# The first layer's input projection as float32 products of unsplit weights and streams

## The chip, the core and the metric

The kernel runs on one core of one Trainium2 chip. The metric is the device time of one execution in microseconds, the median of several runs. The core's engines have queues of their own: PE (TensorE, matmuls; PEld is its weight load), DVE (VectorE), ACT (ScalarE), POOL (GpSimd) and SP (SyncE, which here only issues DMAs). Each engine takes its instructions in the order in which the program holds them, and waits for the data of the one at its head.

## The reference

Two streams, the latent one (512 tokens) and the context (256 tokens), of 1024 channels pass two layers. Of a layer only this matters here:

```python
ul = split_cols(modulate(rms_norm(h_l, norm1_g[i]), m_l[0], m_l[1]) @ w_in[i])
uc = split_cols(modulate(rms_norm(h_c, norm1_g[i]), m_c[0], m_c[1]) @ w_in[i])
# four mixers on slices of the 2696 columns: SSD, Hyena, retention, S5
y_l = jnp.concatenate([ssd_l, hy_l, ret_l, s5l], axis=-1) @ w_out[i]
h_l = h_l + m_l[2] * y_l
h_l = h_l + m_l[5] * swiglu(modulate(rms_norm(h_l, norm2_g[i]), m_l[3], m_l[4]), ffn_w_up[i], ffn_w_down[i])
```

The m are the modulation, six vectors of 1024 channels that a product of a condition with `mod_w` gives. All is float32. The context takes the same path in the first layer; in the second it only feeds the mixers.

## The kernel before

The streams lie with channels on partitions, eight tiles of 128 channels by 512 or 256 tokens. Large products are made as three float32r matmuls: operand and weight are each split into a high part, which float32r carries, and a low part, the rest (`split`: the high part is a copy on ACT, line 155, the low part a subtraction on DVE, line 134, or on POOL for some), and `mm3` multiplies high by high, high by low and low by high, summed in one bank of PSUM. All matmuls go through `mm`, line 126, so rows are told apart by their tiles. `ahl`, `alol` are the normed latent stream, `ahc`, `aloc` the context, `whi`, `wlo` the weights; `wd` is the small weight of the eight dt columns, high and low side by side.

A weight comes in pieces of 128 columns: `piece` loads 512 KB by SP (line 207) into a staging tile `wst` of 4 KB a partition, and `weights` splits two pieces into a pair of tiles, tags "wh" and "wl" of the pool `whl`, two places of 8 KB a partition for each tag. The staging ring "st" has three places. The modulation of the first layer (`mod`) loads its own weights (`wm`, two pieces for each 256 columns) through the same ring and multiplies straight from it; its sums need the PSUM ring "md", which has one bank and is also used by the S5 blocks.

The input projection goes by 11 blocks of columns, in the first layer in the order s5, hz, sb, sx, sz, h0, h1, rk, rv, rq, rg: ten of 256 columns and sb, with 128 and dt. `start` norms the inputs by pairs of channel tiles as their modulation arrives, loads the first two blocks' weights (through a staging ring of its own, "stw") and begins their products; `in_proj` does the others for both streams, and from the sixth block on places two or four tiles of columns of the modulation beside each block. `in_s`, `in_h` and `in_r` take the sums out of PSUM and send them to DRAM, from where the mixers read them. s5 is multiplied in halves of 256 tokens, rv with the stream as the stationary operand and 256 columns of weights as the moving one.

The order of the instructions is made by a planner that runs before the kernel does: each has a priority, and the planner places an instruction on its engine when its own model of the chip has it ready. Products of the projections have a priority 300000 later (`bulk`), so that the mixers' matmuls go first. Filters of Hyena, S5, SSD, Hyena, and retention of the context run beside the projection; the output projection begins after them with weights `wo` and tiles `yhl`, `yhc`.

Of the kernel before, what the change touches and what calls it, by code (L numbers as in the profile page):

```python
# [33 lines left out]
def halves(a):  # L34
    """A table as two float32 parts that float32r carries exactly."""
    def keep12(x):
        u = np.ascontiguousarray(x, np.float32).view(np.uint32).astype(np.uint64)
        return ((u + 2047 + ((u >> 12) & 1)) >> 12 << 12).astype(np.uint32).view(np.float32)
    hi = keep12(a)
    return np.ascontiguousarray(np.stack([hi, keep12(a - hi)], 1))  # L40
# [66 lines left out]
class Kern:  # L107
# [7 lines left out]
    def at(self, p):  # L115
        """Instructions in this block get priorities from p on."""
# [44 lines left out]
    def pst(self):  # L161
        """A PSUM bank from the ring of the current flow of work."""
# [5 lines left out]
    def pst2(self, fl="mm+xb"):  # L168
        """As pst, from two rings in turn where no mixer runs."""
        with self.flow(fl):  # L170
            return self.pst()
# [4 lines left out]
    def flow(self, fl, p=None):  # L176
        """Work that takes its banks and small tiles from rings of its own; p: its priority."""
# [10 lines left out]
    def rsq(self, v, n):  # L188
        """v: (128, n) tile, replaced by 1/sqrt(v)."""
# [13 lines left out]
    def piece(self, src, nk, ncol):  # L203
        """src: (128, nk * ncol) of a weight laid out by pieces."""
        pool, tag = self.stage
        st = pool.tile([128, 1024], F32, tag=tag, name="wst", bufs=2 if tag == "stw" else 3)[:, :nk * ncol]
        self.nc.sync.dma_start(st, src)
        return st.rearrange("p (k n) -> p k n", k=nk)

    def weights(self, srcs, nk=8):  # L210
        """Pieces of 128 columns as high and low parts."""
# [7 lines left out]
    def held(self, src):  # L219
        """Four tiles of rows of a weight with all its columns, src: (8, 128, 512)."""  # L220
# [12 lines left out]
    def proj(self, ps, W, c0, m, a, nk=8, order=None):  # L233
        hi, lo = W
# [6 lines left out]
    def bulk(self):  # L241
        """Products that fill the tensor engine come after the mixers' own."""
# [10 lines left out]
    def run(self):  # L253
        nc, tc, A = self.nc, self.tc, self.A
        es = ExitStack()
        with es:
# [7 lines left out]
            self.stage = self.wst, "st"  # L264
            self.body()
# [11 lines left out]
    def put_y(self, s, k, t, c0=0):  # L277
        """Keep tile k of the mixers' output: as operands of the output projection where these have room already."""
# [12 lines left out]
    def ytiles(self, s, p):  # L291
        """Tiles that are not written in the order of their making: each has its own place."""
# [41 lines left out]
    def mod(self, i, c0, c1):  # L334
        """Columns 256*c0 .. 256*c1 of the modulation of layer i."""
# [15 lines left out]
    def mod_vec(self, i, cols, both, p):  # L351
        """As mod for tiles of columns, with a column of the weights a row: products and sums on VectorE.
        The context stream has the tiles in both only."""
# [16 lines left out]
    def gains(self, i, part, s, gat):  # L370
        """(1 + scale) * g for a stream; part is 1 or 4."""
# [4 lines left out]
    def sq_acc(self, s, x, acc, first):  # L376
        """acc += x*x"""
# [7 lines left out]
    def rinv_rows(self, s, accs, scale, c0=0, c1=None):  # L385
        """Per-token 1/sqrt(scale * sum over channels + eps), broadcast to all partitions in PSUM."""
# [14 lines left out]
    def segs(self, s):  # L401
        """Ranges of tokens that are normed one after the other, so that products of one hide the norm of the next."""
# [23 lines left out]
    def start(self):  # L426
        """Norm of the inputs and the first two blocks of columns of the first layer's input projection,
        by pairs of channel tiles as their modulation arrives."""
# [5 lines left out]
        for s in streams:  # L434
            s.a = self.atiles(s)
# [21 lines left out]
        for j in range(4):  # L457
# [5 lines left out]
            if j < 2:  # L463
                self.stage = self.xp, "stw"
                self.in_weights(0, j)
                self.stage = self.wst, "st"
# [3 lines left out]
            for s, jj in ([(sc, 0)] if j == 0 else [(sc, 1), (sl, 0), (sl, 1)] if j == 1 else [(sc, j), (sl, j)]):  # L470
# [4 lines left out]
                for k in range(2 * jj, 2 * jj + 2):  # L475
                    t = self.tile_t(s, "nt")
                    self.mul(t, self.x[s.name][k], pbs[s.name])
                    self.act(t, t, AF.Identity, bias=m[:, k, s.mi:s.mi + 1], scale=g[:, k:k + 1])
                    hi, lo = s.a[0][k], s.a[1][k]
                    self.act(hi, t)  # L480
                    self.sub(lo, t, hi, None if k % 2 else nc.gpsimd)
# [18 lines left out]
    def sirens(self, i, streams, p):  # L500
        """Hidden features of the filters of layer i at all lags: even lags on the first 64 partitions, odd on the rest."""
# [23 lines left out]
    def filters(self, i, s, p, hid):  # L525
        """Spectra of the two filters of layer i for sequence length s.L; kept in DRAM."""
# [7 lines left out]
        for o in range(2):  # L534
# [30 lines left out]
            # the spectra stay unnormalised; the bias is scaled to match  # L565
# [36 lines left out]
    def conv3(self, out, ps, i, wat, step, tl, bat, n):  # L602
        """out = w0 x[t-1] + w1 x[t] + w2 x[t+1] + b from a projection in PSUM."""
# [5 lines left out]
    def hyena(self, i, s, p, F):  # L609
# [14 lines left out]
        for o in range(2):  # L624
# [14 lines left out]
            for ft in range(nft):  # L639
# [3 lines left out]
                for par in range(2):  # L643
                    ps = self.pst()
                    for cs in range(2):
                        # par 0: Ec | Es ; par 1: Os | Oc
# [22 lines left out]
                # P+ = [Pc | Ps] in t1 ; P- = [Ps' | Pc'] in t3  # L669
# [16 lines left out]
            for c in range(2):  # L686
# [3 lines left out]
                for par in range(2):  # L690
                    # par 0: Q1 C + Q2 S ; par 1: Q3 S + Q4 C
# [21 lines left out]
    def early(self, p):  # L713
        """What the S5 matrices of the first layer are made of, later the tables of the retention."""
        return p.tile([128, 32 * self.S_END], F32, tag="early", name="early")

    def causal(self, t, r, nh, fill):
        """Keep i >= j (r = 0) or i <= j (r = 1) of (j, h, i)."""
# [28 lines left out]
    def ret(self, i, s, p):  # L747
# [13 lines left out]
        # states of the chunks  # L761
# [17 lines left out]
        # running states, kept block-diagonal over the two heads of a tile  # L779
# [72 lines left out]
    def ssd(self, i, s, p):  # L852
# [18 lines left out]
        # token-major  # L871
# [14 lines left out]
        # ln dt - acs of the column's token, per (dir, head)  # L886
# [7 lines left out]
        for c in range(nch):  # L894
# [27 lines left out]
            # within the chunk  # L922
# [36 lines left out]
        for c in range(nch):  # L959
            cs = slice(128 * c, 128 * c + 128)  # L960
            # from the states that enter, with the directions on the two halves
# [847 lines left out]
def layout(inputs):  # L1809
    """The inputs in the order in which the kernel reads them."""  # L1810
    g = {n: np.asarray(a) for n, a in inputs.items()}
    A = {}
# [90 lines left out]
```

## Time and profile before

| | |
|---|---|
| median of 3 runs | 1917.36 us (1913.35 to 1920.76) |
| the profiled execution: span | 1919.5 us |
| PE busy over the span | 1790.1 us, 93% |
| PE busy from 46 to 500 us | 396.8 of 454 us |
| DVE busy from 46 to 500 us | 338.1 us |

The profile is of one execution. Its times count from its first instruction, its span is the time between the first and the last, and it lies 2.1 us above the median of the runs. Busy time of PE is the union of its matmuls, whose ends are modelled and overlap. The granted clock is the share of the full clock that TensorE got, 1 at 2.4 GHz and 0.5 at 1.2 GHz.

### The profile page before, as it was taken

What the parts mean: (1) busy time and instruction counts of PE and PEld (TensorE: products, weight loads), DVE (VectorE), ACT (ScalarE), POOL (GpSimd) and SP (SyncE); (2) the same over time, 40 slices, a digit from 0 to 9 for tenths busy, and PEclk for the clock granted to TensorE, in tenths of its full rate; (3) what the DMA queues carried; (4) which work ended last, traced back from release to release, by engine and by line L of the source; (5) the groups of instructions that cost most, each with busy time, mean ns of one, the idle gap of its engine ahead of it and who ended that gap; (6) DMA issues with size and microseconds to landing.
All of it is one profiled execution on the core that took longest, in us unless ns stands there. A gap on an engine that the chain in (4) does not pass through costs nothing.

```text
span 1919.5 us, 28992 instructions
## 1 busy us (share of the span) xinstructions
PE 1790.1 (93%) x10792; PEld 1526.3 (80%) x10792; DVE 1257.5 (66%) x2941; ACT 713.5 (37%) x1390; POOL 207.3 (11%) x273
## 2 busy tenths in 40 slices
PE   3789878898999999999999999989999999999997
PEld 2678767686789888888888989878866888888886
DVE  8788764778858899777665427678576843233336
ACT  4354234555227223212132115514673542222222
POOL 0201121123002000011223000121110000000000
PEclk9899979998899999999999999999997999999998
DMA  6656588765612335656635513565563322222331
GB/s 231 178 138 186 149 180 229 243 192 160 203 56 89 121 123 164 219 190 230 210 113 131 155 44 123 158 207 159 153 201 96 126 73 94 89 96 88 97 101 56
DMA packets 193089, 280.87 MB, mean 146 GB/s; under 512 B 51745, under 2 KB 127837, under 8 KB 192436
## 3 DMA queue, kind: packets, MB, share of 16 engines
q1 hardware_dynamic: 107188, 166.20, 28.5%
q10 hardware_dynamic: 55920, 64.72, 10.9%
q0 software_dynamic: 29840, 48.09, 8.9%
q8 instruction: 85, 1.39, 0.3%
q14 instruction: 56, 0.46, 0.1%
HBM read 235.00 MB, written 43.96 MB: 145 GB/s over the span
## 4 chain that ended last, share of the span: by engine, by line
PE 58%; DVE 11%; issue 8%; DMA 8%; ACT 3%; POOL 1%; ACTq 0%; SPq 0%; DVEq 0%; POOLq 0%
PE ps_mm L126 31%; PE ps_xb L126 20%; PE ps_xa L126 4%; DMA mvw<-in_wmt_dram 4%; PE ps_md L126 2%; DMA wst<-in_wi_dram 1%; ACT L155 1%; DVE mvo L364 1%; DVE wlo L134 1%; DVE gt L134 1%; DVE t L134 1%; DVE g L1499 1%; DVE cst L134 1%; DVE s5tmp L134 1%; ACT whi L155 1%
## 5 line engine op out<-in xcount | busy, mean ns | idle before, releaser
L155 ACT ACTIVATE whi<-wst 128x1024 fp32r<-128x1024 f32 (+3 forms) x226 | 198.9, 917 | 361.5 <-PE ps_mm L126 169.4
L134 DVE TENSOR_TENSOR wlo<-wst,whi 128x1024 fp32r<-128x1024 f32 (+3 forms) x226 | 233.9, 1058 | 83.5 <-ACT whi L155 81.2
L126 PE MATMUL ps_mm<-alol,whi 128*128 128x512 f32 (+1 forms) x688 | 262.7, 383 | 0.4 <-POOL alol L134 0.4
L126 PE MATMUL ps_mm<-ahl,wlo 128*128 128x512 f32 (+1 forms) x688 | 262.3, 382 | 0.0
L126 PE MATMUL ps_mm<-ahl,whi 128*128 128x512 f32 (+1 forms) x688 | 260.9, 383 | 0.3 <-ACT ahl L155 0.2
L126 PE MATMUL ps_mm<-h,whi 128*128 128x512 f32 (+1 forms) x592 | 168.8, 365 | 0.9 <-DVE h L134 0.7
L126 PE MATMUL ps_xb<-ahl,whi 128*128 128x512 f32 (+1 forms) x416 | 154.2, 373 | 3.8 <-ACT ahl L155 3.8
L126 PE MATMUL ps_xb<-ahl,wlo 128*128 128x512 f32 (+1 forms) x416 | 153.8, 370 | 0.0
L126 PE MATMUL ps_xb<-alol,whi 128*128 128x512 f32 (+1 forms) x416 | 153.5, 371 | 0.1
L134 DVE TENSOR_TENSOR sg<-sg,ps_mm 128x512 f32<-128x512 f32 (+1 forms) x70 | 39.9, 570 | 172.9 <-PE ps_mm L126 172.7
L126 PEld LDWEIGHTS ps_mm<-alol,whi 128*128 128x128 f32 x688 | 130.7, 190 | 26.4 <-issue 2.7
L126 PEld LDWEIGHTS ps_mm<-ahl,wlo 128*128 128x128 f32 x688 | 130.7, 190 | 24.5 <-issue 1.1
L126 PEld LDWEIGHTS ps_mm<-ahl,whi 128*128 128x128 f32 x688 | 130.2, 191 | 25.0 <-issue 1.6
L126 PE MATMUL ps_xb<-h,whi 128*128 128x256 f32 (+1 forms) x592 | 129.2, 310 | 0.1
L364 DVE SCALAR_TENSOR_TENSOR mvo<-mvw,crow 128x1024 f32<-128x1024 f32 x80 | 97.8, 1222 | 39.6 <-DMA mvw<-in_wmt_dram 38.7
L126 PE MATMUL ps_mm<-ahc,whi 128*128 128x256 f32 x368 | 107.4, 296 | 13.0 <-ACT whi L155 8.6
L126 PEld LDWEIGHTS ps_mm<-h,whi 128*128 128x128 f32 x592 | 103.7, 188 | 17.5 <-DVE h L134 1.2
L126 PE MATMUL ps_mm<-aloc,whi 128*128 128x256 f32 x368 | 108.2, 295 | 1.0 <-DVE aloc L134 1.0
L126 PE MATMUL ps_mm<-ahc,wlo 128*128 128x256 f32 x368 | 107.1, 293 | 2.0 <-DVE wlo L134 2.0
L126 PEld LDWEIGHTS ps_xb<-h,whi 128*128 128x128 f32 x592 | 98.9, 188 | 11.6 <-issue 1.1
L126 PE MATMUL ps_mm<-h,wlo 128*128 128x512 f32 (+1 forms) x296 | 107.9, 365 | 0.0
L155 ACT ACTIVATE h<-sg 128x512 fp32r<-128x512 f32 (+1 forms) x70 | 37.4, 534 | 161.7 <-DVE sg L134 161.6
(576 smaller groups left out, 4137.3 us busy)
## 6 DMA issues: line engine op xcount, KB each, us to landing
wst<-in_wu_dram SPq DMA_DIRECT2D x88, 512.0 KB
mvw<-in_wmt_dram POOLq DMA_DIRECT2D x56, 512.0 KB, 3.7
wst<-in_wi_dram SPq DMA_DIRECT2D x42, 512.0 KB
wst<-in_wm_dram SPq DMA_DIRECT2D x40, 512.0 KB
wst<-in_wd_dram SPq DMA_DIRECT2D x24, 384.0 KB
ftab<-in_c_ftL_dram POOLq DMA_DIRECT2D x32, 256.0 KB, 5.0
wst<-in_wd_dram SPq DMA_DIRECT2D x32, 256.0 KB
s5rot<-s5r SPq DMA_DIRECT2D x32, 192.0 KB
```

Of the source, the lines that this page charges most:

```text
L126: return self.nc.tensor.matmul(out, lhsT, rhs, start=start, stop=stop)
L134: return (eng or self.nc.vector).tensor_tensor(out, a, b, op=op)
L155: return self.nc.scalar.activation(out, in_, func, bias=bias, scale=scale)
L364: self.nc.vector.scalar_tensor_tensor(o, st, 1.0, crow[:, q], op0=ALU.mult, op1=ALU.mult, accum_out=mv[:, c, q:q + 1])
L1499: nc.vector.tensor_tensor_scan(o, dcy, x, 0.0, ALU.mult, ALU.add)
```

## The change

In the first layer the normed streams are no longer split: the norm's activation writes eight float32 tiles for each stream (the pool `ap` has 8 tiles of each instead of 16). The weights of the input projection are not split either: `plain` loads each piece by SP straight into one of the four places of the tags "wh" and "wl", taken in turn, with no staging. `proj` then makes one float32 product for each tile of rows. The dt weights become one padded tile of 64 columns in a place of its own. The second layer is as before, and the ring "stw" is gone.

```diff
+    def plain(self, srcs):
+        self.nplain += 1
+        w = self.whl.tile([128, 8, 256], F32, tag=("wh", "wl")[self.nplain % 2], name="wpl")
+        for h, src in enumerate(srcs):
+            self.nc.sync.dma_start(w[:, :, 128 * h:128 * h + 128], src.rearrange("p (k n) -> p k n", k=8))
+        return w
...
     def proj(self, ps, W, c0, m, a, nk=8, order=None):
+        if len(a) == 1:
+            with self.bulk():
+                for k in range(nk):
+                    self.mm(ps, W[:, k, c0:c0 + m], a[0][k], k == 0, k == nk - 1)
+            return
...
-            s.a = self.atiles(s)
+            s.a = [[self.ap.tile([128, s.L], F32, tag="a" + s.name, name="af" + s.name) for _ in range(8)]]
...
-                self.stage = self.xp, "stw"
                 self.in_weights(0, j)
-                self.stage = self.wst, "st"
...
-                    self.act(t, t, AF.Identity, bias=m[:, k, s.mi:s.mi + 1], scale=g[:, k:k + 1])
-                    hi, lo = s.a[0][k], s.a[1][k]
-                    self.act(hi, t)
-                    self.sub(lo, t, hi, None if k % 2 else nc.gpsimd)
+                    self.act(s.a[0][k], t, AF.Identity, bias=m[:, k, s.mi:s.mi + 1], scale=g[:, k:k + 1])
...
-        self.Ws[q] = self.weights([wi[:, 8 * o:8 * o + 1024] for o in range(off, off + ncol - 127, 128)])
+        self.Ws[q] = (self.weights if i else self.plain)([wi[:, 8 * o:8 * o + 1024] for o in range(off, off + ncol - 127, 128)])
...
+                            o = ps[:, 256 * j:256 * j + 256]
+                            if i == 0:
+                                self.mm(o, s.a[0][k][:, cs], W[:, k, :], k == 0, k == 7)
+                                continue
...
+        if i == 0:
+            self.nplain += 1
+            wd = self.wd = self.whl.tile([128, 8, 256], F32, tag=("wh", "wl")[self.nplain % 2], name="wdp")[:, :, 0:64]
+            self.nc.gpsimd.memset(wd, 0.0)
+            for r in range(2):
+                self.act(wd[:, :, 32 * r:32 * r + 4], st[:, :, 4 * r:4 * r + 4])
+            return
...
+                if i == 0:
+                    self.mm(ps[0:64, :n], self.wd[:, k], s.a[0][k], k == 0, k == 7)
+                    continue
...
+        if i == 0:
+            self.ts(dt, ps[0:64, :n], self.dtb[i], op0=ALU.add)
+        else:
+            self.act(t1, ps[64:128, :n])
+            self.stt(dt, ps[0:64, :n], self.dtb[i], t1, ALU.add, ALU.add)
...
-            self.ap = aps.enter_context(tc.tile_pool(name="ap", bufs=16, reuse_waits="tile"))
+            self.ap = aps.enter_context(tc.tile_pool(name="ap", bufs=16 if i else 8, reuse_waits="tile"))
```

## Rows read from the trace of the kernel before

**Rows 1.** Busy time (share of the span) and instructions, the page.

```profile
...
PE 1790.1 (93%) x10792; PEld 1526.3 (80%) x10792; DVE 1257.5 (66%) x2941; ACT 713.5 (37%) x1390; POOL 207.3 (11%) x273
...
```

**Rows 2.** Busy by stretch: PE, PEld, DVE, ACT, POOL, clock, DMA share, GB/s.

```profile
...
100.00:225.00 125.00, 118.12 (x749) 98.95 (x748) 107.56 (x250) 61.14 (x122) 14.66 (x15) 0.99 0.60 161
225.00:300.00 75.00, 53.74 (x317) 43.70 (x319) 44.95 (x100) 22.36 (x46) 14.42 (x19) 0.77 0.82 189
300.00:350.00 50.00, 46.45 (x317) 37.48 (x309) 27.07 (x51) 28.14 (x49) 5.76 (x6) 1.00 0.81 225
350.00:375.00 25.00, 21.25 (x164) 17.79 (x166) 21.27 (x43) 15.26 (x42) 9.15 (x10) 0.86 0.64 208
...
46.00:500.00 454.00, 396.82 (x2641) 327.89 (x2634) 338.14 (x773) 204.12 (x427) 84.10 (x92) 0.91 0.66 183
...
457.00:498.00 41.00, 32.43 (x236) 25.46 (x234) 35.01 (x107) 15.06 (x34) 5.86 (x10) 0.74 0.49 153
...
```

**Rows 3.** Busy time in stretches, of instructions on whi alone.

```profile
...
249.00:278.60 29.60, 0.00 (x0) 0.00 (x0) 0.58 (x1) 1.06 (x1) 0.66 0.61 168
...
```

**Rows 4.** SP's issues in order; its waits (225 to 300): total, times, longest.

```profile
...
270.34 0.34 SPq L207 DMA_DIRECT2D wst<-in_wi_dram  x1
...
SPq L207 <- PE ps_md L126: 10.4, 2, 9.9
...
```

**Rows 5.** PE's waits from 30 to 480 us: total, times, longest.

```profile
...
PE ps_xa L126 <- DVE rv L152: 9.1, 1, 9.1
PE ps_mm L126 <- ACT whi L155: 8.6, 1, 8.6
PE ps_xb L126 <- ACT sE L155: 5.5, 1, 5.5
...
PE ps_mm L126 <- ACT ahc L155: 4.0, 2, 3.4
...
```

**Rows 6.** Matmuls by tiles, 46 to 458 us: busy, mean ns, idle before.

```profile
...
L126 PE MATMUL ps_mm<-ahl,whi 128*128 128x512 f32 x136 | 56.3, 414 | 0.1
...
L126 PE MATMUL ps_mm<-ahc,whi 128*128 128x256 f32 x136 | 41.1, 312 | 13.0 <-ACT whi L155 8.6 <-ACT ahc L155 4.0 <-DVE BC L152 0.5
...
L126 PE MATMUL ps_mm<-whi,ahl 128*128 128x256 f32 x32 | 9.4, 301 | 0.0
...
L126 PE MATMUL ps_mm<-ahl,wd 128*128 128x512 f32 x8 | 3.3, 415 | 0.0
...
```

**Rows 7.** PE in order of time (start us, us); the matmuls that read glw.

```profile
...
103.12 0.39 PE L126 MATMUL ps_mm<-alol,whi 128*128 128x512 f32 x1
...
105.87 0.39 PE L126 MATMUL ps_mm<-alol,whi 128*128 128x512 f32 x1
...
204.15 0.28 PE L126 MATMUL ps_mm<-aloc,whi 128*128 128x256 f32 x1
...
205.80 0.28 PE L126 MATMUL ps_mm<-ahc,whi 128*128 128x256 f32 x1
...
282.89 0.59 PE L126 MATMUL ps_xa<-s5fy,glw 128*128 128x256 f32 x2
...
283.44 0.28 PE L126 MATMUL ps_mm<-aloc,whi 128*128 128x256 f32 x1
...
L126 PE MATMUL ps_xa<-s5fy,glw x40: 377/379/795, 282.9 to 1382.2; 128*128 128x256 f32 x40
...
```

**Rows 8.** Splits of the weights to 432 us: duration min/median/max, first and last.

```profile
...
L155 ACT ACTIVATE whi<-wst x21: 1041/1057/1062, 22.3 to 404.8; 128x1024 fp32r<-128x1024 f32 x21
...
L134 DVE TENSOR_TENSOR wlo<-wst,whi x21: 1193/1224/2185, 24.4 to 405.9; 128x1024 fp32r<-128x1024 f32 x21
...
```

**Rows 9.** PE by time: first and last projection product, first output product.

```profile
...
46.61 0.80 PE L126 MATMUL ps_mm<-ahc,whi 128*128 128x256 f32 x2
...
456.89 0.28 PE L126 MATMUL ps_mm<-ahc,wlo 128*128 128x256 f32 x1
...
498.21 0.79 PE L126 MATMUL ps_mm<-yhl,whi 128*128 128x512 f32 x1
...
```

More of the change, by code (lines that the diff above doesn't have):

```diff
@@ L205, in piece @@
         pool, tag = self.stage
-        st = pool.tile([128, 1024], F32, tag=tag, name="wst", bufs=2 if tag == "stw" else 3)[:, :nk * ncol]
+        st = pool.tile([128, 1024], F32, tag=tag, name="wst", bufs=3)[:, :nk * ncol]
         self.nc.sync.dma_start(st, src)
         return st.rearrange("p (k n) -> p k n", k=nk)
+    def plain(self, srcs):
[4 more added lines that the diff above has]
+        return w
     def weights(self, srcs, nk=8):
@@ L264, in run @@
             self.stage = self.wst, "st"
+            self.nplain = 0
             self.body()
@@ L1015, in in_weights @@
         wi = self.A["wi"][i]
-        self.Ws[q] = self.weights([wi[:, 8 * o:8 * o + 1024] for o in range(off, off + ncol - 127, 128)])
+        self.Ws[q] = (self.weights if i else self.plain)([wi[:, 8 * o:8 * o + 1024] for o in range(off, off + ncol - 127, 128)])
         if nm == "sb":
-            self.dt_weights(wi[:, 8 * (off + 128):8 * (off + 136)])
+            self.dt_weights(i, wi[:, 8 * (off + 128):8 * (off + 136)])
     def in_part(self, i, q, s):
@@ L1089, in in_r @@
                         for k in range(8):
-                            self.mm3(ps[:, 256 * j:256 * j + 256], s.a[0][k][:, cs], s.a[1][k][:, cs],
+                            o = ps[:, 256 * j:256 * j + 256]
+                            if i == 0:
+                                self.mm(o, s.a[0][k][:, cs], W[:, k, :], k == 0, k == 7)
+                                continue
+                            self.mm3(o, s.a[0][k][:, cs], s.a[1][k][:, cs],
                                      W[0][:, k, :], W[1][:, k, :], k == 0, k == 7)
@@ L1118, in in_r, with dt_weights @@
             self.out_raw(s.drk[:, at + c], t)
-    def dt_weights(self, src):
+    def dt_weights(self, i, src):
         st = self.sm.tile([128, 8, 8], F32, tag="dtw", name="dtw", bufs=1)
         self.nc.sync.dma_start(st, src.rearrange("p (k n) -> p k n", k=8))
+        if i == 0:
[5 more added lines that the diff above has]
+            return
         wd = self.wd = self.whl.tile([128, 8, 256], F32R, tag="wh", name="wd")[:, :, 0:128]
@@ L1156, in ssd_in @@
         nc.sync.dma_start(scanm, A["c_scan"][:, :n])
-        self.act(t1, ps[64:128, :n])
-        self.stt(dt, ps[0:64, :n], self.dtb[i], t1, ALU.add, ALU.add)
+        if i == 0:
[3 more added lines that the diff above has]
+            self.stt(dt, ps[0:64, :n], self.dtb[i], t1, ALU.add, ALU.add)
         self.act(t1, dt, AF.Abs)
```

## The prediction

> **What bounds the kernel now.** I read the page first [rows 1]: over its 1919.5 us span PE is busy 93%. That share mixes two things, so the second view cuts the span into stretches [rows 2]. The change touches only the first layer's input projection, whose products lie on PE from 46.6 to 457 us [rows 9], so the stretch to look at is 46 to 500. There PE is busy 396.8 of 454 us: it idles 57.2 us and holds a granted clock of 0.91. The reader should see that the loss is uneven. From 225 to 300 PE is busy only 53.7 of 75 us at clock 0.77; at the two levels of 1.2 and 2.4 GHz a mean of 0.77 means 46% of that stretch, 34.5 us, at the lower one. DVE has 338 of 454 us, and in 300 to 350 only 27.1 of 50. So the stretch is mostly bound by PE, with a hole in the middle and a tail (457 to 498) in which DVE is busy 35.0 of 41 us.
>
> The hole is what matters. Between 249 and 278.6 us PE runs not one product that reads a weight tile whi [rows 3]. The code and the queue of SP say why. The staging ring "st" has three places, shared by the modulation weights (wm) and the projection weights (wi). wm loads take the places first; the modulation's products must wait for the one PSUM bank of ring "md", which the S5 blocks use too. Until then the ring is full of wm: SP stands 10.4 us waiting for PE's ps_md products, and the next wi load is issued at 270.3 [rows 4]. PE then waits 8.6 us for the split of that weight [rows 5].
>
> **Added: longer products.** The projection has 136 products of 512 columns, 168 + 64 of 256, and 8 + 8 for dt, each now issued as three float32r matmuls (dt: two). The lines view has 136 for ahl and 136 for ahc in ring mm, 32 for the S5 halves of the latent stream [rows 6]; the remaining 64 = 32 + 16 + 16 stand in like rows: 1136 matmuls in all. Start to start, a 512-column float32r matmul takes (105.87 - 103.12) / 12 = 0.229 us over a run of twelve, so 0.6875 a product; a 256-column one (205.80 - 204.15) / 14 = 0.118 over fourteen, 0.354 a product [rows 7]. The price of a float32 product is on the trace too: the GLU's weight glw and its stream are float32, and its 20 products (three ranges of tokens in the first layer, two in the second, by two tiles of columns and two of rows) show as 40 matmuls, two each. From the first of two at 282.89 to 283.44 there are those two and one float32r matmul: 0.55 - 0.118 = 0.432 us for one float32 product of 256 columns [rows 7]. No float32 product of 512 columns is in the trace. From above I bound it by twice that, 0.864, since nothing that is paid once a matmul can double; from below by the ratio that float32r shows between the two widths, 0.432 x 0.229 / 0.118 = 0.84. I take 0.864; the lower bound would make the sum 3 us smaller.
> - 136 x (0.864 - 0.6875) = 24.0 us
> - 232 x (0.432 - 0.3536) = 18.2 us
> - dt: 8 x (0.864 - 0.458) + 8 x (0.432 - 0.236) = 4.8 us
>
> Together +47 us of PE at full clock. The Trainium skill (FP8 and Floating Point Precision, TensorE Precision Notes) speaks against the change more strongly: true FP32 takes four passes through the array. By it every product would cost 4/3 of today's three; the trace has 0.432 against 0.354 at 256 columns, 1.22 times. By the page the 512-column products, which the trace doesn't show, would add another 136 x (0.917 - 0.864) = 7 us to the sum; it is a rival below.
>
> **Removed on DVE, ACT and POOL.** 21 splits of weight pieces: 1.06 us on ACT and 1.22 us on DVE each [rows 8], 22 and 26 us. The 16 casts of the normed streams on ACT and their 16 subtractions on DVE and POOL go as well. dt loses one ACT copy and two small subtractions, its DVE add stays. All of it lies beside PE work except at these places:
>
> Start. Four of the 21 DVE splits (4 x 1.22 = 4.9 us), those of the first two blocks, come from 24.4 us on [rows 8], ahead of the norm's rv, for which PE waits 9.1 us [rows 5]. They come off that chain. From there to 100 us PE waits 4.0 us for ahc [rows 5]; the norm's activation now writes the operand itself, so I take 3 back. **-8** (bounds -5 and -11).
>
> Hole. Weights go straight from DRAM to four places of 8 KB (tags wh and wl, two each), one place a column block, dt's padded columns taking one. The load of a block waits for the products of the block four tiles earlier, not for st. So the blocks after h0 no longer wait for the modulation. The 21.3 us of idle time in 225 to 300 contain the 8.6 for whi, which goes; the rest are waits of the S5 chain (KT through DRAM, gt), which stay where the program's order puts PE behind them. I take 14. With products to run PE would also keep its clock: the 34.5 us at the lower level, of which it is busy 53.7 / 75, some 24.7, lose half of that, 12.4; I take 10. **-24** (bounds -8.6, the one direct wait, and -34).
>
> Elsewhere from 100 to 457. PE waits 5.5 us for sE, an activation queued on ACT behind the split of a weight that had just landed [rows 5], and the stretch 350 to 375 has clock 0.86 [rows 2], 7 us at the lower level, worth 3. With 1.5 of the 6.9 us that PE idles in 100 to 225: **-10** (bounds 0 and -14).
>
> Tail. Today's last projection product starts at 456.9, the first of the output projection at 498.2 [rows 9]; between them PE runs what is left of Hyena, SSD and the context's retention at clock 0.74, behind DVE (35.0 of 41 us) [rows 2]. Hyena and SSD need blocks (h1 above all) that the hole holds back to 278 us and later. If they are there earlier, their DVE work moves into 300 to 350, where DVE has 23 us free. I take half of the tail's DVE work, 17.5, with its little idle time: **-18** (bounds 0 and -30). This is the least certain term.
>
> DMA. Bytes are the same, but a load now lands in eight runs of 512 B a partition instead of one of 4 KB. DMA's share is 0.66 in this stretch [rows 2]. Lower bound nothing, since a load has up to three blocks' time; upper, one more late load like the 8.6 us one. I take 0. SP issues the same 21 loads, with no staging wait, but a load whose place is still read stands at the head of SP with the S5 loads (KT, s5U) behind it: a rival. The smaller pool of streams (8 tiles instead of 16) can only take waits away from the retention's pools laid over it: 0.
>
> **Sum.** 47 - 8 - 24 - 10 - 18 = -13 us. The profiled execution spans 1919.5 us, 2.1 above the median of 1917.4 and inside the three runs (1913.4 to 1920.8), so I take the difference to the median: **1904 us**. What runs after 500 us is not touched.
>
> **Rivals.**
> - The tail does not move (its chains are latencies, or they wait for rq and rg, which still come last): 47 - 8 - 24 - 10 = +5, 1922 us, within 0.5%. For it: retention of the context starts only when the last product has freed the streams. Against: DVE, not latency, fills the tail. Chance 0.25.
> - Slower: PE's instruction order is fixed beforehand, and the longer products do not land in the hole but ahead of mixers' matmuls that are ready. Then only the direct wait of 8.6 comes back there and the tail stays: 47 - 8 - 8.6 - 10 = +20, 1938 us. It decides as soon as hole and tail together give back less than 47 - 18 - 9.6 = 19 us. For it: 100 to 225 is full already, 118.1 of 125 us [rows 2], so what is added there has no cover at its own place. Chance 0.18.
> - SP's head: a wi load waiting for its place holds back KT and s5U, as the wm loads did for 10.4 us [rows 4]. Two and a half such stretches on the S5 chain, some 25 us: -13 + 25 = +12, 1929 us. Against: four places are more than the two pairs of today. Chance 0.08.
> - A float32 product of 512 columns costs 4/3 of its three float32r matmuls, 0.917 us instead of 0.864: -13 + 7 = -6, 1911 us, within 0.5%. This is what the Trainium skill's page would make of it. The 0.432 us at 256 columns speak against it. Chance 0.05.
>
> **Chances and range.** The forecast (-13, its own range 1885 to 1907) has 0.44. A kernel like this is told from no change at about 0.5%, 9.6 us. Faster 0.44; same 0.25 + 0.05 = 0.30; slower 0.18 + 0.08 = 0.26. Adding up the bounds gives +33 and -42; 8 in 10 is 1885 (the hole at its bound of -34 and the tail at -27) to 1938 (the slower rival).
>
> **What the changed profile would show.** Right: 768 projection matmuls instead of 1136, those of 512 columns about 0.43 apart; no whi or wlo before 430 us; projection products all through 249 to 278; clock in 225 to 300 above 0.9; last projection product near 450, first output product at 475 to 490, and the shift equal to the gain. Wrong if float32 matmuls of 512 columns stand further apart than 0.43, if PE idles as long as now in the S5 chain while weights lie ready, or if SP shows long waits for PE at the wpl loads.

## The result and the profile after

The changed kernel is slower: 1940.7 us (1933.2 to 1942.7) against 1915.4 us for the kernel before on the same chip, 1.0116 times with a 95% interval of 1.0090 to 1.0143: 25 us by the medians, 22 by that ratio, which compares the means of the runs. The forecast was 13 us faster, and the time lies 2.7 us above the upper end of the range. The profiled execution spans 1941.0 us, 21.5 more than before.

The profile after, busy times of the page (answering to [rows 1]):

```profile
PE 1823.9 (94%) x10424; PEld 1490.2 (77%) x10424; DVE 1227.4 (63%) x2910; ACT 686.2 (35%) x1351; POOL 198.3 (10%) x265
```

Its stretches (answering to [rows 2], with the same columns):

```profile
...
225.00:300.00 75.00, 70.35 (x351) 48.96 (x350) 44.66 (x104) 24.50 (x49) 13.28 (x17) 0.98 0.79 185
300.00:350.00 50.00, 50.00 (x256) 32.35 (x255) 22.65 (x45) 23.13 (x45) 7.95 (x8) 1.00 0.82 235
...
46.00:500.00 454.00, 415.92 (x2154) 279.29 (x2153) 297.41 (x700) 174.85 (x379) 75.14 (x84) 0.95 0.64 174
457.00:498.00 41.00, 25.84 (x169) 19.88 (x168) 34.00 (x83) 10.64 (x30) 12.50 (x16) 0.75 0.28 88
```

The hole is filled: PE is busy 70.35 of the 75 us from 225 on at clock 0.98, against 53.74 at 0.77 [rows 2]. Between 300 and 350 it doesn't idle at all. Yet from 457 to 498 it does less than before, 25.84 us instead of 32.43. PE in order of time, the projection's price and both ends of the tail (answering to [rows 7, 9]; an x2 row is one product):

```profile
446.91 1.02 PE L126 MATMUL ps_mm<-afl,wpl 128*128 128x512 f32 x2
447.77 1.03 PE L126 MATMUL ps_mm<-afc,wpl 128*128 128x256 f32 x4
448.63 0.27 PE L640 MATMUL ps_xb<-const,hin 128*128 128x128 f32 x1
...
513.23 2.05 PE L126 MATMUL ps_xa<-const,rv 128*128 128x128 f32 x8 [2.52 <-DVE rv L152]
520.70 0.79 PE L126 MATMUL ps_mm<-yhl,whi 128*128 128x512 f32 x1 [5.41 <-ACT yhl L155]
```

One product of 512 columns takes 447.77 - 446.91 = 0.86 us, one of 256 columns (448.63 - 447.77) / 2 = 0.43: the forecast had 0.864 and 0.432. The projection's last products run at 448, 8 us earlier than before, and the first product of the output projection at 520.7, 22.5 us later [rows 9]. That is the whole loss in time (what holds that product back is another question; see e5). From it PE works 102 us without a gap up to the feed-forward, in both kernels. Before (first fence) and after, the stretches up to the first output product and the one behind it, without those shown already:

```profile
0.00:46.00 46.00, 14.72 (x88) 8.25 (x92) 38.62 (x242) 21.37 (x47) 1.49 (x7) 1.00 0.65 235
46.00:225.00 179.00, 161.30 (x1044) 134.97 (x1037) 147.87 (x346) 79.78 (x160) 26.29 (x26) 0.95 0.60 163
...
300.00:450.00 150.00, 140.35 (x1014) 116.75 (x1007) 101.41 (x202) 81.43 (x172) 35.61 (x34) 0.98 0.69 209
450.00:498.00 48.00, 39.43 (x267) 30.76 (x265) 41.92 (x121) 19.33 (x47) 7.78 (x14) 0.75 0.50 158
498.00:600.00 102.00, 101.88 (x737) 89.94 (x734) 74.74 (x191) 39.98 (x90) 5.02 (x7) 0.99 0.41 135
...
```

```profile
0.00:46.00 46.00, 20.23 (x111) 12.25 (x112) 38.29 (x250) 18.59 (x46) 1.23 (x7) 1.00 0.79 251
46.00:225.00 179.00, 164.46 (x771) 105.91 (x771) 125.70 (x309) 62.09 (x127) 17.45 (x17) 0.94 0.64 167
...
300.00:450.00 150.00, 148.72 (x832) 100.74 (x831) 86.66 (x190) 70.79 (x161) 31.91 (x34) 1.00 0.66 199
450.00:521.00 71.00, 45.40 (x293) 35.32 (x292) 50.28 (x130) 21.03 (x51) 12.50 (x16) 0.72 0.37 114
521.00:623.00 102.00, 101.90 (x731) 90.20 (x731) 73.52 (x186) 39.57 (x89) 5.03 (x7) 0.98 0.40 131
```

These rows put numbers on every term of the forecast. In each stretch, busy time times mean clock is taken as the work at full clock, and the rest as lost (rough, since the mean clock is that of the whole stretch, rounded to 0.01, which is worth up to 1 us).

| term | forecast | measured |
|---|---|---|
| longer products (work at full clock, to the first output product) | +47 | +49 |
| start (0 to 46) | -8 | -5.5 |
| hole (225 to 300) | -24 | -27.6 |
| elsewhere (46 to 225, 300 to 450) | -10 | -12.5 |
| tail (from 450) | -18 | **+19.9** |
| sum | -13 | +23 |

Example of the working: the hole lost 75 - 53.74 x 0.77 = 33.6 us before and 75 - 70.35 x 0.98 = 6.1 after. Four terms are within 4 us. The fifth is off by 38 us and has the wrong sign.

What ends later is the mixers' chain. ACT's queue shows three of its points; before (first fence) and after: the last S5 block's output, the start of the latent stream's SSD, its end (the stores of its result). The fence of after also has the rows that the text below speaks of.

```profile
267.98 0.31 ACT L155 ACTIVATE ys<-ps_md 128x192 f32<-128x192 f32 x1
...
395.17 0.32 ACTq L864 DMA_DIRECT2D sin<-dss0l  x1
...
493.25 0.98 ACTq L281 DMA_DIRECT2D yd0l<-sin  x2
```

```profile
281.40 0.31 ACT L155 ACTIVATE ys<-ps_md 128x192 f32<-128x192 f32 x1
...
403.43 0.33 ACTq L873 DMA_DIRECT2D sin<-dss0l  x1
...
459.27 0.60 ACT L155 ACTIVATE sE<-ps_xb 128x512 f32<-128x512 f32 x1 [2.45 <-PE ps_xb L126]
...
461.18 0.44 ACT L155 ACTIVATE sdec<-E 64x4 f32<-64x4 f32 x2
...
516.18 0.98 ACTq L295 DMA_DIRECT2D yd0l<-sin  x2
...
518.70 1.43 ACT L155 ACTIVATE yhc<-yl 128x256 fp32r<-128x256 f32 x4 [9.76 <-issue]
```

S5 is 13 us late where the hole used to be, SSD starts 8 us late and ends 23 us late. Where in the SSD the rest is lost shows at its last load of E (a table of decays), at the activation of it (sdec), at the last update of its state (Hn), and at the loads of the keys of the context's retention (rk), the mixer that must wait until the projection has released the streams. Before and after:

```profile
444.07 0.38 SPq L897 DMA_DIRECT2D E<-acd0l  x1
...
450.12 0.44 ACT L155 ACTIVATE sdec<-E 64x4 f32<-64x4 f32 x2 [1.05 <-POOL t L134]
...
461.29 0.48 ACTq L755 DMA_DIRECT2D rk<-drk0c  x1
...
470.38 0.42 DVE L134 TENSOR_TENSOR Hn<-Hn,sS 64x256 f32<-64x256 f32 x1
```

```profile
449.53 0.37 SPq L906 DMA_DIRECT2D E<-acd0l  x1
...
453.83 0.33 ACTq L764 DMA_DIRECT2D rk<-drk0c  x1
...
490.41 1.30 DVE L134 TENSOR_TENSOR Hn<-Hn,sS 64x256 f32<-64x256 f32 x1
```

The last load of E is 5.5 us late. So 17 of the 23 us are lost behind it, when the projection's products, the last of which end at 449, are off PE. E had landed at 455.6, but sdec stands in ACT's order behind an activation of Hyena (sE), which waits for Hyena's products on PE: 11 us late. The last Hn is 20 us late: from sdec to it DVE works 10.9 us for the context's retention (tiles ve, qe, rH, rHf, sd, ry), where before it was 1.5 us (ve, qe). The projection's earlier end lets that retention load its keys 7.5 us earlier, while the SSD comes later, and so the two meet on DVE. This is read from the rows; no run changes that order alone.

The splits of the output projection's operands (yhc) come right behind the SSD's stores, before which ACT does nothing for 9.8 us.

### The profile page after: what moved, and what is told of

It is laid out like the page before. It is cut to its first block, busy times and chain, and to the rows that moved or that the text cites. A ratio compares the mean times of both kernels' runs of the same rounds, so it can differ in the third digit from the quotient of the medians.

```text
span 1941.0 us, 28177 instructions
## 1 busy us (share of the span) xinstructions
PE 1823.9 (94%) x10424; PEld 1490.2 (77%) x10424; DVE 1227.4 (63%) x2910; ACT 686.2 (35%) x1351; POOL 198.3 (10%) x265
## 3 DMA queue, kind: packets, MB, share of 16 engines
q10 hardware_dynamic: 55920, 64.72, 10.9%
## 4 chain that ended last, share of the span: by engine, by line
PE 64%; DVE 12%; DMA 11%; issue 9%; ACT 3%; POOL 1%; ACTq 0%; SPq 0%; DVEq 0%; POOLq 0%
PE ps_mm L126 33%; PE ps_xb L126 22%; PE ps_xa L126 5%; DMA mvw<-in_wmt_dram 5%; PE ps_md L126 3%; DVE mvo L378 1%; DVE cst L134 1%; ACT L155 1%; DMA s5r<-cst 1%; DMA sin<-dss1l 1%; ACT E L155 1%; DMA s5m<-s5M 0%; DVE s5tmp L134 0%; DVE s5tq L134 0%; DVE s5M L134 0%
## 5 line engine op out<-in xcount | busy, mean ns | idle before, releaser
L134 DVE TENSOR_TENSOR wlo<-wst,whi 128x1024 fp32r<-128x1024 f32 (+3 forms) x205 | 208.4, 1043 | 64.6 <-ACT whi L155 63.1
L126 PE MATMUL ps_mm<-alol,whi 128*128 128x512 f32 (+1 forms) x552 | 207.2, 377 | 0.4 <-POOL alol L134 0.4
L126 PE MATMUL ps_mm<-ahl,wlo 128*128 128x512 f32 (+1 forms) x552 | 206.7, 375 | 0.0
L126 PE MATMUL ps_mm<-ahl,whi 128*128 128x512 f32 (+1 forms) x552 | 204.2, 375 | 0.1
L126 PE MATMUL ps_mm<-afl,wpl 128*128 128x512 f32 x272 | 128.8, 605 | 0.0
L126 PEld LDWEIGHTS ps_mm<-alol,whi 128*128 128x128 f32 x552 | 104.5, 189 | 19.9 <-issue 1.0
L126 PEld LDWEIGHTS ps_mm<-ahl,wlo 128*128 128x128 f32 x552 | 104.4, 189 | 19.1 <-issue 0.6
L126 PEld LDWEIGHTS ps_mm<-ahl,whi 128*128 128x128 f32 x552 | 103.4, 189 | 18.8 <-issue 0.4
L126 PE MATMUL ps_xb<-h,wlo 128*128 128x256 f32 (+1 forms) x296 | 91.7, 310 | 0.0
L152 DVE SCALAR_TENSOR_TENSOR xl<-ps_mm,modv,xl 128x512 f32<-128x512 f32 (+1 forms) x84 | 54.0, 646 | 54.8 <-PE ps_mm L126 54.7
```

What stands on the lines that cost most here:

```text
L126: return self.nc.tensor.matmul(out, lhsT, rhs, start=start, stop=stop)
L134: return (eng or self.nc.vector).tensor_tensor(out, a, b, op=op)
L152: return self.nc.vector.scalar_tensor_tensor(out, a, s, b, op0=op0, op1=op1)
```

## The experiments

Three theories came up in turn. A: the added volume on PE decides. B: weights that are ready early let the projection run ahead of the mixers on PE, and the mixers end later. C: what must end is a path through the latent SSD and the retention behind it, not the projection. Ratios are to the kernel before on the same chip, with 95% intervals.

**e1, e3: volume with the old loads.** e1 keeps the float32 products but loads the weights through the staging rings and copies them; e3 keeps the products of before and takes two of the eight tiles of rows twice (an output that counts them twice), which brings about the change's added time. The first diff is e1's, on the changed kernel, the second e3's, on the kernel before.

```diff
-            self.nc.sync.dma_start(w[:, :, 128 * h:128 * h + 128], src.rearrange("p (k n) -> p k n", k=8))
+            self.act(w[:, :, 128 * h:128 * h + 128], self.piece(src, 8, 128))
...
```

```diff
...
+            ks = order or list(range(nk)) + ([0, 1] if self.twice else [])
...
```

> Float32 products as in the change, but the weights come as before through the staging rings and are copied by ACT into the same four places (no direct load). Theory A (the 47 us of longer products are the cause: PE is full from 241 to 450 us and the mixers' matmuls wait in its queue): as slow as the change or slower, 1935 to 1950 us. Theory B (the weights that lie ready early let the projection run ahead of the mixers, and the price matters less): the hole comes back and gives the mixers their free run, 1915 to 1925 us.

> The kernel before (float32r, staged loads, splits) with two of the eight row tiles multiplied twice in the first layer's input projection (its sums are therefore others): PE volume 10/8 x 180 = 225 us, that of the change. Theory A: slower than before by 15 to 30 us, 1930 to 1945. Theory B: the volume goes into idle PE time, 1915 to 1925 us.

e1: 1948.5 us, 1.0178 (1.0139 to 1.0218). e3: 1944.7 us, 1.0149 (1.0118 to 1.0180). With the old loads the projection ends at 486 and 489 us, some 30 us later than before, and the context's retention, which needs the streams released, loads its keys at 489 and 491 us instead of 461. Both times lie where A had put them, and B's 1915 to 1925 missed: volume does cost where it delays that. By the ratios the early weights of the change win back some 12 us of it (8 by the medians; the intervals overlap a little, and e1 has the copies on ACT as well). The hole did not come back as expected: PE is busy 67.7 (e1) and 66.3 (e3) of the 75 us from 225 on. And in e1 S5 ends at 255 us, 13 earlier than before, yet the latent SSD ends at 515: a late S5 isn't needed for a late SSD.

**e2, e4: early weights without volume.** e2 is the change with six of the eight tiles of rows (a quarter of the first layer's input projection is left out); e4 is the kernel before with the modulation columns that filled the staging ring put behind later blocks. Again the first diff is on the changed kernel, the second on the kernel before.

```diff
-                for k in range(nk):
-                    self.mm(ps, W[:, k, c0:c0 + m], a[0][k], k == 0, k == nk - 1)
+                for k in range(6):
+                    self.mm(ps, W[:, k, c0:c0 + m], a[0][k], k == 0, k == 5)
...
```

```diff
-            if i == 0 and 5 <= q < 11:
+            if i == 0 and 7 <= q < 11:
                 with self.at(prio + 2000 * q + 1000):
-                    self.mod(0, 2 * q - 2, 2 * q)
+                    self.mod(0, 3 * q - 13, 3 * q - 10)
```

> The change with 6 of the 8 row tiles of each product of the first layer's input projection (it leaves out a quarter of that product): PE volume of the projection 6/8 x 227 = 170 us, somewhat under the 180 us of before, and the direct loads kept. Theory A: the loss goes and the time is that of before or less, 1890 to 1915 us. Theory B: still slower than before, 1925 to 1940 us.

> The kernel before with only the place of the modulation's second part moved: its columns 8 to 19 stand behind blocks rk to rg, three at a time, instead of behind h0 to rg, two at a time, so that the weights of h1 and rk take the staging ring ahead of it and the hole at 249 to 278 us is filled with float32r products. The prediction's terms for hole and tail: faster by 10 to 40 us, 1875 to 1905. Theory B (what fills the hole delays S5 and Hyena): no gain or slower, 1912 to 1930 us.

e2: 1929.2 us, 1.0071 (1.0048 to 1.0094). e4: 1935.9 us, 1.0110 (1.0077 to 1.0142). This is the telling pair: the projection ends at 408 and 429 us, 49 and 28 us earlier than before, and both are slower. The latent SSD ends 12 and 15 us later than before. A alone falls, and what B says of the times holds (e4 lies even above its range). Two things weaken B's mechanism, products ahead of the mixers on PE. In e4 the hole of before is filled, but another opens behind it:

```profile
225.00:300.00 75.00, 70.41 (x449) 59.27 (x448) 50.02 (x111) 26.27 (x54) 15.71 (x21) 0.98 0.83 188
300.00:350.00 50.00, 39.78 (x274) 31.00 (x273) 21.96 (x43) 26.38 (x44) 5.11 (x5) 0.80 0.72 212
```

In e2 the mixers run in another order: the context's retention loads its keys at 409 us and the latent SSD its inputs only at 425 (395 before), with PE idle for 10.8 of the 50 us from 400 on. There the SSD isn't shown to wait behind the projection on PE; what is shown is that an earlier projection alone gains nothing.

**e5, e6: the first output product comes free.** The SSD's tiles lie on the other side of the memory, so that the operands of the output projection don't take over their places.

```diff
-                with self.rp("ssdl") as p2, self.flow("xa", chunk((4, 2)[i])):
+                with (self.rp("ssdl") if i else tc.tile_pool(name="ssdl", bufs=1, reuse_waits="tile")) as p2, \
+                        self.flow("xa", chunk((4, 2)[i])):
```

> The changed kernel; only the tiles of the latent stream's SSD of the first layer lie on the other side of the memory, so that the tiles of the output projection's operands no longer take over their places. Theory C (the first output product waits for the end of that SSD, because its operands take over the SSD's memory): the first output product comes some 3 us after the end of the latent Hyena (about 509 us), near 512 instead of 521, and the time falls to 1930 to 1935 us. Rival D (the splits stand behind the SSD's stores in ScalarE's queue, wherever the tiles lie): the first output product stays at 519 to 522 us, the time at 1937 to 1943 us.

> The same move of the SSD's tiles in the kernel before. Theory C: the latent Hyena ends at 485 us there, so the first output product can come near 490 instead of 498, and the time falls to about 1907 to 1911 us. Rival D: no change, 1912 to 1918 us.

e5: 1943.5 us, 1.0123 (1.0098 to 1.0149). e6: 1916.2 us, 0.9994 (0.9980 to 1.0008). In e5 the mechanism worked and the time did not move. ACT, e5:

```profile
510.37 1.15 ACT L155 ACTIVATE yhl<-yl 128x512 fp32r<-128x512 f32 x2 [2.75 <-DMA yd0l<-hx]
...
520.33 0.99 ACTq L295 DMA_DIRECT2D yd0l<-sin  x2
...
523.31 0.44 ACTq L764 DMA_DIRECT2D rk<-drk0l  x1
```

The splits (and the first output product, 511) come 10 us earlier, so it was the memory of the SSD that held them. In e6 that product comes at 495, 3 us earlier. But the feed-forward still starts at 622 us. What did not move is the SSD's end and, behind it, the loads of the latent stream's retention. The first output product is not what sets the end: the part of theory C that I held then fell.

**e7, e8, e17, e18: part of the projection behind the mixers.** The weights of the last blocks (rq and rg in e7; rv too in e8; rg alone in e17), with the modulation columns beside them, are loaded behind a load of the latent SSD's E: the third, in e18 (rq and rg) the second.

```diff
-            self.in_proj(i, PB)
+            self.in_proj(i, PB, 0, 11 if i else 9)
...
                     self.ssd(i, sl, p2)
+                if i == 0:
+                    with tc.issue_after(self.eload[2]):
+                        self.in_proj(i, PB, 9, 11)
```

> The changed kernel; the weights of the projection's last two blocks (rq, rg) and the four columns of modulation beside them are loaded behind the third load of E of the latent SSD (about 441 us). Theory B (bulk products that lie ahead of the mixers' own on TensorE between 225 and 450 us delay the mixers): some 21 us of products move out of 400 to 450 into TensorE's idle time after 450, the latent SSD ends near 508 instead of 517, and the time falls to 1928 to 1935 us. Rival (the volume of products decides, or retention's later inputs do): the mixers end where they did or the projection's end becomes the last wait, 1938 to 1948 us.

> As the run with two blocks, with rv held too, three blocks and some 31 us of products. Theory B: the latent SSD ends near 503 to 508, the time is 1925 to 1935 us unless the retention of the context, which needs rv, becomes the last to end. Rival: 1940 to 1955 us, with the wait at the output projection's second part.

> As e7, with only the last block (rg, about 10 us of products) held behind the third load of E. Two paths: the latent SSD ends near 508 to 512 us (517 changed, 500 with two blocks), so the retention's last split near 586 to 590; the projection ends near 465 to 475, so the context's retention starts 12 to 20 us later than in the changed kernel. If both count as read: 1930 to 1940 us. If only the volume of products counts: 1940 to 1948 us.

> As e7, with both last blocks held behind the second load of E (about 417 us) instead of the third: the projection ends near 470 to 480 us. Two paths: the latent SSD ends near 505 to 510, the context's retention starts near 475: 1933 to 1945 us, between the changed kernel and e7 or below both. If only the volume counts: 1940 to 1950 us.

e7: 1953.2 us, 1.0184 (1.0161 to 1.0208). e8: 1991.0 us, 1.0386 (1.0355 to 1.0418). e17: 1946.9 us, 1.0130 (1.0082 to 1.0178). e18: 1948.8 us, 1.0146 (1.0112 to 1.0181). The SSD ended earlier, as B says, but no time came where B had put it: e17 and e18 lie in their rivals' ranges, e7 and e8 above both. e7, ACT, and PE's stretch that was emptied:

```profile
500.09 0.98 ACTq L296 DMA_DIRECT2D yd0l<-sin  x2
...
504.74 0.44 ACTq L765 DMA_DIRECT2D rk<-drk0l  x1
...
506.53 0.33 ACTq L765 DMA_DIRECT2D rk<-drk0c  x1
```

```profile
350.00:450.00 100.00, 81.77 (x466) 59.50 (x465) 61.48 (x152) 39.39 (x111) 24.34 (x26) 0.85 0.58 182
```

With PE busy 81.8 instead of 98.7 us in these 100 us, the SSD's stores come at 500 instead of 516 us. (The held modulation may have a share in that, and so may the context's retention, which in these runs comes behind the SSD: they can't tell the projection's products on PE from the retention's work on DVE.) But now the context's retention, whose places are those of the streams, loads its keys only at 506.5, 3 us after the projection's last product, instead of 454. The same in e17 (504 and 491) and e18 (496 and 497): in these three one path gains 12 to 20 us and the other loses 37 to 53.

**e9 to e12: the retention's own bank.** The latent retention takes PSUM from the modulation's ring instead of the two banks that the SSD uses before it; e10 and e12 move the SSD's tiles as well.

```diff
-                    with self.flow("xa", chunk(1)):
+                    with self.flow("md", chunk(1)):
                         self.ret(i, sl, p3)
...
-                    ps = self.pst2("mm+mm+md")[:, :s.L]
+                    ps = self.pst2("mm")[:, :s.L]
```

> The changed kernel; the latent stream's retention of the first layer takes its products' bank from the modulation's ring (one bank) instead of the two that the latent SSD uses before it, and the output projection's first part keeps to the main ring. Theory C2 (what sets the end is that retention: 518 to 596 us in the changed kernel, 495 to 573 before, 78 us in both, and it starts when the latent SSD leaves its banks): it starts once the streams are released (about 455 to 470 us), its last split falls from 596 to 575 us or less, then the context's path decides, and the time falls to 1924 to 1933 us. Rival (VectorE, 40 of 50 us busy between 450 and 500, is what the mixers share, and one bank makes the retention longer): retention takes from the SSD what it gains, 1937 to 1946 us.

> As the run with the retention's own bank, and the SSD's tiles on the other side of the memory as well, so that the output projection's first part can start near 511 us. Theory C2: both paths come earlier, 1914 to 1926 us. Rival: 1937 to 1946 us.

> The same bank for the latent retention in the kernel before. Theory C2: before has two paths of one length there (the retention's last split 573 us, the context's part from 548 us, both leading to the latent part at 576 us), and TensorE is idle for some 9 of the 50 us from 450; the retention's products fill part of that, so the output projection's first part meets fewer of them: 1903 to 1912 us. Rival: 1914 to 1922 us.

> Both moves in the kernel before. Theory C2: 1898 to 1909 us, below both kernels. Rival: 1913 to 1922 us.

e9: 1945.1 us, 1.0151 (1.0138 to 1.0164). e10: 1949.3 us, 1.0172 (1.0159 to 1.0185). e11: 1927.0 us, 1.0054 (1.0041 to 1.0067). e12: 1924.0 us, 1.0048 (1.0034 to 1.0061). Theory C's numbers miss in all four, and only e9 lies in its rival's range: the retention starts no earlier than the SSD lets it (its keys load at 517.5 us in e9, 491 in e11), so the banks don't tie it to the SSD. With one bank it takes longer, and this shows the other half. Its last splits, changed kernel and e9:

```profile
L155 ACT ACTIVATE yhl<-ry x2: 630/630/631, 595.4 to 596.3; 128x512 fp32r<-128x512 f32 x2
```

```profile
L155 ACT ACTIVATE yhl<-ry x2: 629/630/632, 606.1 to 608.9; 128x512 fp32r<-128x512 f32 x2
```

In e9 they are 12.6 us later and the output projection's second part for the latent stream starts 13 us later, at 612 instead of 599, though the context's came 8 us earlier. In e11 the same: 12 us later (585), and the time goes up by some 10 us.

**e13 to e16: the retention's loads and places.** e13 (on e9) issues its three loads from GpSimd's queue, e14 adds second places for its score and query tiles; e15 is the kernel before with these places alone, e16 the kernel before with bank, queue and places.

```diff
+        ld = nc.gpsimd if lat and not i else nc.scalar
...
-        nc.scalar.dma_start(kk, s.drk[:, 0:2])
+        ld.dma_start(kk, s.drk[:, 0:2])
...
-            qe = p.tile([128, 2, 2, 128], F32, tag="qe", name="qe", bufs=2 if i else 1)
+            qe = p.tile([128, 2, 2, 128], F32, tag="qe", name="qe", bufs=2 if i or lat else 1)
```

> As the changed kernel with the retention's own bank (e9, 1945 us); its three loads stand in GpSimd's queue instead of ScalarE's. If ScalarE's queue ties the retention's start to the SSD's stores: the loads come at 455 to 495 us instead of 518, the last split falls from 609 to 575 to 590 us, time 1925 to 1938 us. If not: the loads move but the retention's first products still come after 517 us, 1940 to 1948 us.

> As e13, with two places instead of one for the retention's score and query tiles (sd, qe), so that its four chunks overlap. If the end follows the retention's last split: below e13 by what that split moves, 3 to 12 us. Otherwise the same time as e13.

> The kernel before with the two places for sd and qe alone. Two paths of one length end there (retention's last split 573 us, the context's second part leading to 576 us): if both count, shortening one gives at most 1 to 4 us, 1911 to 1917 us.

> The kernel before with the retention's own bank, its loads in GpSimd's queue and the two places. If the link holds: the retention's last split falls below 573 us (585 with its own bank alone), the output projection's first part meets fewer of its products, 1900 to 1914 us. If not: 1920 to 1930 us as with its own bank alone.

e13: 1946.2 us, 1.0159 (1.0136 to 1.0181). e14: 1948.1 us, 1.0169 (1.0145 to 1.0194). e15: 1916.9 us, 1.0004 (0.9986 to 1.0022). e16: 1925.4 us, 1.0063 (1.0035 to 1.0091). e13, e14 and e16 came where they were expected if there is no such link, e15 at the slow end of its range. The loads moved, the work didn't. e13, GpSimd and then ACT:

```profile
492.21 0.54 POOL L765 DMA_DIRECT2D rk<-drk0l  x1
```

```profile
519.53 0.98 ACTq L295 DMA_DIRECT2D yd0l<-sin  x2
...
532.56 0.38 ACT L155 ACTIVATE kt<-ps_md 128x256 f32<-128x256 f32 x1 [1.94 <-PE ps_md L776]
```

Keys that were issued at 492 us are used first at 532, 12 us behind the SSD's stores; in e16 they were issued at 464 and used at 504. So neither these banks nor these loads alone tie the retention to the SSD. In e13 its first products stand on PE behind the first of the output projection (523.6); whether the planner's order, memory places or another engine puts them there stays open. No run was faster than the kernel before.

**All runs in one table** (us, read from the traces: end of the projection's last product; first store of the latent SSD; start of the retention's last split; first update of the output projection's second part, context and latent; first SiLU of the feed-forward). The ratio is that of the times.

| run | projection | SSD | retention | 2nd part, context | 2nd part, latent | feed-forward | ratio |
|---|---|---|---|---|---|---|---|
| before | 457 | 493 | 573 | 548 | 576 | 600 | 1 |
| changed | 449 | 516 | 596 | 571 | 599 | 623 | 1.012 |
| e1 | 486 | 515 | 599 | 574 | 602 | 626 | 1.018 |
| e2 | 408 | 505 | 586 | 561 | 588 | 612 | 1.007 |
| e3 | 489 | 498 | 584 | 583 | 594 | 620 | 1.015 |
| e4 | 429 | 508 | 588 | 563 | 591 | 615 | 1.011 |
| e5 | 450 | 520 | 595 | 570 | 598 | 622 | 1.012 |
| e6 | 454 | 490 | 572 | 547 | 575 | 599 | 0.999 |
| e7 | 504 | 500 | 586 | 594 | 604 | 631 | 1.018 |
| e8 | 531 | 497 | 618 | 626 | 637 | 663 | 1.039 |
| e9 | 448 | 516 | 609 | 563 | 612 | 632 | 1.015 |
| e10 | 451 | 521 | 613 | 565 | 616 | 636 | 1.017 |
| e11 | 451 | 490 | 585 | 537 | 588 | 608 | 1.005 |
| e12 | 455 | 494 | 589 | 542 | 592 | 612 | 1.005 |
| e13 | 449 | 520 | 612 | 567 | 616 | 635 | 1.016 |
| e14 | 450 | 520 | 613 | 567 | 616 | 636 | 1.017 |
| e15 | 452 | 490 | 571 | 546 | 574 | 598 | 1.000 |
| e16 | 453 | 492 | 585 | 539 | 588 | 608 | 1.006 |
| e17 | 487 | 504 | 587 | 584 | 596 | 624 | 1.013 |
| e18 | 494 | 496 | 590 | 589 | 600 | 626 | 1.015 |

The second part for the latent stream starts at the later of two: retention + 3 or context + 11, within 1 us in every row. In the kernel before that is 576 against 559. By this fit the projection's side had 17 us to spare, and making the projection end earlier could give nothing; e2 and e4 agree. From there to the feed-forward it is 20 to 28 us, least where the context is far ahead (e9 to e14, e16), so the fit doesn't cover that last piece.

## Why the prediction was wrong

- **Price of the products: right.** 0.86 and 0.43 us against 0.864 and 0.432; +49 us of work against +47. The rival with 4/3 of today's price, an estimate from the four passes of the Trainium skill (FP8 and Floating Point Precision, TensorE Precision Notes), is out: the 512-column product, which only this trace shows, takes 0.86 us and not 0.917. That speaks against the estimate, which took each of the three float32r matmuls for one pass; whether there are four passes no run shows.
- **Start, hole, elsewhere: right** within 4 us each; the hole's clock of 0.98 came as forecast. So did the projection's last product (448, forecast near 450). SP's head, a rival there, is out too; SP's waits of the changed kernel (40 to 450 us; total, times, longest) have 6.4 us for places of the weights, and still the modulation's:

```profile
SPq L207 <- PE ps_md L126: 100.7, 16, 14.4
...
SPq L215 <- PE ps_mm L126: 6.4, 3, 2.9
```

- **Tail: the step that failed.** The prediction said that the mixers' "DVE work moves into 300 to 350, where DVE has 23 us free" once their blocks come earlier, and took 18 us back. Its bounds, 0 and -30, allowed no loss there. No such move was measured: DVE does 22.65 us in 300 to 350, where it did 27.07 before [rows 2], of which 3.7 are splits that are gone, and the tail lost 20 us more. Weights that lie ready earlier did not bring the mixers forward. Their work is chains that pass PE, ACT, DVE and GpSimd in turn, each engine in a fixed order. With the hole filled, S5 came 13 us later (10 in e4) and the latent SSD's last E 5.5 us later; in the tail itself another 17 us went, behind Hyena on ACT and beside the context's retention on DVE. Which of these queues is worth how much no run separates, so the cause within the chains stays open.
- **What was not asked: which path ends last.** The tail was read as something between two PE products. The table shows two paths, and in the kernel before, by the fit under it, the one through the latent SSD and its retention was already the later by 17 us. What the projection saved did not count; what the SSD lost counted in full: +23 us at its stores, +23 at the feed-forward, +25 in the time.
- **The rivals.** The slower one (PE's order is fixed beforehand, longer products land ahead of the mixers' matmuls, 1938 us) came within 3 us of the time, by luck: it expected the hole to give back 8.6 us and the tail to stay. The hole gave back 27.6 and the tail took 19.9, two errors that cancel. Longer products do cost (e1, e3), but e2 and e4 lose without them.
- **Signs.** None of the three signs of being wrong came, and the signs of being right held up to the projection's last product. The one behind it, at the step that failed, did not: the first output product came at 520.7 instead of 475 to 490.

## What to carry to other kernels

An idle stretch of the bulk engine may be the time in which latency chains on other engines run; before filling it, follow the path that ends the stage and ask what the filled-in work puts in front of it, on every engine and not only on the one that is filled. Count a saving only as far as its own path is the last one: here the side that was improved had 17 us to spare. One trace shows the two paths; how far each lies from the end took runs in which the other was the later. A wait that ends last (the first output product) need not be the one that counts: freeing it (e5) gave nothing.

## What the runs showed of the hardware

- A float32 product shows as two matmuls; at full clock one product takes 0.86 us for 512 columns and 0.43 for 256, against 0.6875 and 0.354 for three float32r matmuls: 1.25 and 1.22 times.
- The tail pays twice for PE's idle time, in both kernels: with PE busy 45 of the 71 us from 450 on (39 of 48 before) the granted clock is 0.72 (0.75), and the first output products still run at the lower level of 1.2 GHz, those of 256 columns 0.21 us apart (starts at 521.29, 521.50, 521.72; before at 498.80, 499.02, 499.23) where 0.118 is the pitch at 2.4 GHz [rows 7].
- With weight loads that land in eight runs of 512 B a partition DMA's share from 46 to 500 us is 0.64 at 174 GB/s, before 0.66 at 183 [rows 2]; SP's waits for the weights' places are 6.4 us. No cost of the short runs was seen.
